# Decoder trunk: a pair's last product one place forward, the fourth-sum product first at second pairs, and a part's last modulation row moved into the next part

## The chip, the cores and the metric

One core of one Trainium2 chip runs the program. The metric is the device time of one execution in microseconds (us), lower being better; three timed executions of the kernel before lie between 1927.19 and 1928.88.

Names used for the engines: PE is TensorE (matrix products), DVE is VectorE, ACT is ScalarE, POOL is GpSimd, SP is SyncE, which here only issues transfers.

## The reference, cut to what matters

Two layers over x (512 tokens by 1024 features). Each layer is a half-step feed-forward block (FFN), a token mixer (a short gated convolution in layer 0, sparse attention in layer 1) and a second half-step FFN, so there are four FFNs. The change touches only the FFNs and the modulation rows that are computed beside them.

```python
def swiglu(h, w_in, w_out):
    g, u = jnp.split(h @ w_in, 2, axis=-1)
    return (jax.nn.silu(g) * u) @ w_out

cond = jax.nn.silu(c)
for i in range(DEPTH):
    mod = (cond @ ada_w[i] + ada_b[i]).reshape(bsz, 3, 3, D_MODEL)
    shift, scl, gate = mod[:, :, 0], mod[:, :, 1], mod[:, :, 2]
    h = adaln(x, norm_g[i, 0], shift[:, 0], scl[:, 0])
    x = x + HALF * gate[:, 0, None, :] * swiglu(h, ffn_w_in[i, 0], ffn_w_out[i, 0])
    ...  # the mixer, then the second FFN in the same way
```

`w_in` is 1024 by 5632 (gate and up halves of 2816 each), `w_out` is 2816 by 1024, and `ada_w` is 1024 by 9216 for each layer.

## The kernel before, in words

Every float32 product is made as three products of rounded float32r operands: `mm3` (L166 to L169) multiplies the high part of the weights by the high and by the low part of the activations, and the low part of the weights by the high part. An operand is split into its high and low part by `split` (L162 to L164): ACT writes the high part, and DVE subtracts it from the source for the low part. So each weight tile passes through ACT and then DVE (tiles `whi`, `wlo`; `qah`, `qal`; `qbh`, `qbl`; `qch`, `qcl`; `qdh`, `qdl`) before PE can use it.

An FFN (`ffn`, L620) works through the 22 column blocks of the hidden layer. A block j holds a gate column and an up column of 128 features, a *pair*. The blocks are cut into four *parts* (`FOUR`: blocks 0 to 5, 6 to 11, 12 to 17, 18 to 21). After a part's pairs, that part's share of the second matrix is multiplied (tiles `y`, weights `in_ffo`) and added to x, eight output rows d (L806); the last part does this in two halves (tiles `ty`).

A pair is computed by `seven_products` (L634): a scheme of Strassen's kind that makes the pair's four half-size blocks with seven half-size products. Each product is 4 `mm3`, 12 matmuls of 128x256. In program order a pair brings these, with the PSUM tiles `ox`, `oy`, `oz` and the copies of their sums into SBUF (`e`, `e3`):

1. first weights `a11` (tile `whi`/`wlo`) into `ox`, copied by ACT to `e`;
2. `before[0]()`, which is the *fourth* product of the pair before (`b4`, tiles `qdh`/`qdl`, into that pair's `oy`, then DVE L718 and ACT L719);
3. second weights `a12` (the other half of `whi`/`wlo`) into `oz`, added by DVE L705;
4. `b2` (`qbh`/`qbl`) into `ox` again, copied by ACT to `e` (the copy that the variable `copy` keeps);
5. `s1` (`qah`/`qal`) into `oy`, copied by ACT to `e3`;
6. `before[1]()`, the *last* product of the pair before (`c22`, tiles `qch`/`qcl`, into that pair's `ox`), then DVE L724 and L725, which read `ox` and make the pair's hidden activation `af`, and `keep`, which splits it (`ahi`, `alo`; `hid.done` holds the two instructions);
7. `s3` (`qah`/`qal`) into `ox`, added by DVE L714.

The first pair of a part has nothing to do at 2 and 6. The last pair's fourth and last products are made after the loop, among the first `y` products. At the second pair of a part (`second`, worked out in the loop of L756 on as "the block after the first one") the split of `whi` waits for the copy of the pair before (`issue_after`, L663).

The sums `qb` of DVE (L661, L662) are made from the raw weight tile `wraw` (3 buffers) and the accumulated tile `qa`; SP loads `wraw`, two halves of `qa` and `a22` for each pair (L647, L648, L656, L657), and POOL adds the fourth block to `qa` with an accumulating transfer (L654). A load waits until its buffer is free.

The modulation rows (`adaraw`, one row of `ada_w` for 128 features) are spread over the FFN: `each()` does the next one. It issues a 512 KB load into one of two buffers (L153, from POOL in these FFNs) and then `row_sum` on DVE (L147, an instruction of 128x1024 that multiplies by `cond` and sums, and one that reads the sum). Rows are asked for once before the `y` stage (`row()`) and after each output row d's addition L806 in the first three parts of an FFN (in the first FFN not in its first part, except d from 2 to 6). The fourth FFN has none.

Each engine runs its instructions in the order in which a scheduler has written them; the scheduler goes by program order, priorities and `issue_after`, and its order may differ from program order.

## Time and profile before

| what | value |
|---|---|
| median of three timed runs | 1927.41 us |
| the profiled execution's own time | 1933.05 us |
| its span, first to last instruction | 1931.3 us |
| PE busy | 1881.0 us (97%) |
| DVE busy | 1515.2 us (78%) |
| ACT busy | 950.9 us (49%) |
| POOL busy | 250.6 us (13%) |
| mean granted TensorE clock | 0.998 |
| transfers | 324.76 MB, mean 168 GB/s |
| chain of waits, shares | PE 74%, DVE 13%, DMA 7%, ACT 3% |

In a row of the timeline stand the start in us from the span's start, the duration, the engine, the line, the operation, output and inputs, and in brackets how long the engine was idle before it and what released it. The row of a wait gives the total in us, the number of times and the longest one. A row of a windows table gives busy time and number of instructions of PE, weight loads, DVE, ACT and POOL, then the granted clock, the transfer engines' share and GB/s.

### The profile page before, as it was taken

Reading aid. Unit: us, or ns where it says so; the run is one execution under the profiler, and the core shown is the slowest. Engines: PE = TensorE matmul, PEld = TensorE weight load, DVE = VectorE, ACT = ScalarE, POOL = GpSimd, SP = SyncE. Lnnn points to the kernel's source line nnn. Section 1 sums busy time; section 2 is a strip of 40 time slices with the busy share of each in tenths; the row PEclk is TensorE's granted clock in tenths of the full one; section 3 lists DMA queues with packets and bytes.
Section 4 is the critical chain, followed back from the end, with each engine's and each line's share of the span. In section 5 each row is a group of like instructions: output and inputs, shape, how many; then the busy total and the mean of one; then the engine's idle time right before and its main releaser. Section 6 shows DMA issues by size and latency. Waiting matters only on the chain.

```text
span 1931.3 us, 34417 instructions
## 1 busy us (share of the span) xinstructions
PE 1881.0 (97%) x13293; PEld 1742.4 (90%) x13293; DVE 1515.2 (78%) x2792; ACT 950.9 (49%) x1679; POOL 250.6 (13%) x346
## 2 busy tenths in 40 slices
PE   7999999999999999999999999999999999999999
PEld 5989898988899898989989898999888789898989
DVE  8976768888798777788878777787898988585765
ACT  3445353543236353535636353554788856363532
POOL 0010101000020111110011111000354620010100
PEclk9999999999999999999999999999999999999999
DMA  8576677457666676774567675324333325474741
GB/s 327 186 225 175 208 186 224 156 174 268 228 178 168 205 198 208 186 229 121 145 215 195 211 204 193 105 90 141 77 98 87 92 67 144 124 187 120 202 118 63
DMA packets 126673, 324.76 MB, mean 168 GB/s; under 512 B 15515, under 2 KB 16651, under 8 KB 126508
## 3 DMA queue, kind: packets, MB, share of 16 engines
q1 hardware_dynamic: 95196, 242.85, 38.5%
q0 software_dynamic: 31312, 79.71, 18.3%
q8 instruction: 104, 1.70, 0.4%
q14 instruction: 61, 0.50, 0.1%
HBM read 313.85 MB, written 3.15 MB: 164 GB/s over the span
## 4 chain that ended last, share of the span: by engine, by line
PE 74%; DVE 13%; DMA 7%; ACT 3%; issue 3%; SPq 1%; POOL 0%; DVEq 0%; ACTq 0%; POOLq 0%
PE gu L169 11%; PE gu L167 11%; PE gu L168 11%; PE y L167 5%; PE y L169 5%; PE y L168 5%; DMA adaraw<-in_adaw 2%; DVE wlo L164 2%; PE cv L167 2%; PE cv L168 2%; PE cv L169 2%; DMA wraw<-in_ffi 2%; PE ty L168 2%; PE ty L167 2%; PE ty L169 2%
## 5 line engine op out<-in xcount | busy, mean ns | idle before, releaser
L163 ACT ACTIVATE whi<-wraw 128x1024 fp32r<-128x1024 f32 (+2 forms) x261 | 252.9, 976 | 266.4 <-PE y L168 89.6
L164 DVE TENSOR_TENSOR wlo<-wraw,whi 128x1024 fp32r<-128x1024 f32 (+2 forms) x261 | 294.9, 1135 | 44.3 <-ACT whi L163 43.5
L169 PE MATMUL y<-ahi,wlo 128*128 128x512 f32 x576 | 224.3, 389 | 0.8 <-DVE wlo L164 0.8
L168 PE MATMUL y<-alo,whi 128*128 128x512 f32 x576 | 224.3, 389 | 0.0
L167 PE MATMUL y<-ahi,whi 128*128 128x512 f32 x576 | 224.3, 389 | 0.0
L147 DVE CUSTOM_DVE_ANT_0 adaraw<-adaraw,cond,adabs 128x1024 f32<-128x1024 f32 x144 | 185.2, 1303 | 40.3 <-DMA adaraw<-in_adaw 40.1
L169 PE MATMUL gu<-hhi,wlo 128*128 128x256 f32 x696 | 195.0, 280 | 14.1 <-DVE wlo L164 13.9
L167 PE MATMUL gu<-hhi,whi 128*128 128x256 f32 x696 | 193.8, 278 | 3.8 <-DVE af L725 3.8
L168 PE MATMUL gu<-hlo,whi 128*128 128x256 f32 x696 | 193.1, 278 | 0.0
L654 POOL DMA_DIRECT2D qa<-in_ffi x70 | 84.5, 1207 | 723.6 <-DMA qa<-in_ffi 248.0
L697 ACT ACTIVATE e<-gu 128x256 f32<-128x256 f32 x219 | 82.8, 378 | 168.4 <-PE gu L169 168.3
L167 PE MATMUL gu<-th,qah 128*128 128x256 f32 x584 | 161.4, 276 | 0.8 <-ACT e L697 0.8
L168 PE MATMUL gu<-tl,qah 128*128 128x256 f32 x584 | 161.3, 276 | 0.0
L169 PE MATMUL gu<-th,qal 128*128 128x256 f32 x584 | 161.3, 276 | 0.0
L169 PEld LDWEIGHTS gu<-hhi,wlo 128*128 128x128 f32 x696 | 131.1, 188 | 17.2 <-DVE wlo L164 17.2
L167 PEld LDWEIGHTS gu<-hhi,whi 128*128 128x128 f32 x696 | 131.1, 188 | 5.3 <-DVE af L725 4.8
L168 PEld LDWEIGHTS gu<-hlo,whi 128*128 128x128 f32 x696 | 131.0, 188 | 0.5
L169 PEld LDWEIGHTS y<-ahi,wlo 128*128 128x128 f32 x576 | 108.1, 188 | 24.2 <-DVE wlo L164 1.5
L167 PEld LDWEIGHTS y<-ahi,whi 128*128 128x128 f32 x576 | 108.2, 188 | 21.6
L168 PEld LDWEIGHTS y<-alo,whi 128*128 128x128 f32 x576 | 108.1, 188 | 21.6
L167 PEld LDWEIGHTS gu<-th,qah 128*128 128x128 f32 x584 | 109.7, 188 | 1.0 <-ACT e L697 1.0
L169 PEld LDWEIGHTS gu<-th,qal 128*128 128x128 f32 x584 | 109.7, 188 | 0.0
(327 smaller groups left out, 5753.8 us busy)
## 6 DMA issues: line engine op xcount, KB each, us to landing
wraw<-in_ffi SPq DMA_DIRECT2D x103, 512.0 KB, 4.7
adaraw<-in_adaw POOLq DMA_DIRECT2D x79, 512.0 KB, 4.8
qa<-in_ffi SPq DMA_DIRECT2D x146, 256.0 KB, 3.8
wraw<-in_ffo SPq DMA_DIRECT2D x96, 384.0 KB, 4.3
qa<-in_ffi POOLq DMA_DIRECT2D x70, 512.0 KB, 6.7
adaraw<-in_adaw SPq DMA_DIRECT2D x65, 512.0 KB, 4.6
a<-in_ffi SPq DMA_DIRECT2D x73, 256.0 KB, 4.4
wraw<-in_cwi SPq DMA_DIRECT2D x24, 512.0 KB, 4.5
```

What stands on the lines that cost most here:

```text
L147: return nc.vector.tensor_tensor_reduce(out=raw, in0=raw, in1=cond, scale=scale, scalar=adabs[:, c:c + 1], op0=ALU.mult, op1=ALU.add, accu ...
L163: act = nc.scalar.activation(hi, src, AF.Copy)
L164: return act, nc.vector.tensor_tensor(lo, src, hi, ALU.subtract)
L167: nc.tensor.matmul(o, sh, mh, start=first, stop=False, **kw)
L168: nc.tensor.matmul(o, sh, ml, start=False, stop=False, **kw)
L169: nc.tensor.matmul(o, sl, mh, start=False, stop=last, **kw)
L654: nc.gpsimd.dma_start(qa, bass.AP(tensor=a21.tensor, offset=a21.offset, ap=[a21.ap[0], [0, 2], a21.ap[1]]), accum_op=ALU.add)
L697: return nc.scalar.activation(to, o[:, lo], AF.Copy)
```

## The change

Three edits in `seven_products` and the loop that calls it:

- Products 5 and 6 change places: `before[1]()`, the last product of the pair before, comes ahead of `s1`. The split of `a22` into `qch`/`qcl`, which reuses the buffer that this product reads, goes with it.
- At a part's second pair, `before[0]()`, the fourth product of the first pair, comes ahead of product 1 in place of behind it.
- In parts whose rows follow every d, the row after d = 7 is not done there. Its d is put on a list `late`, and the row is done in the next part's second pair, after `before[1]()`, ordered behind the split of that pair's hidden activation. The number of rows stays the same. Eight rows are moved: two in the first FFN and three in each of the second and third; in the fourth, where no rows are left, the call does nothing.

```diff
--- before.py
+++ after.py
@@ -696,20 +696,27 @@
                     with tc.high_priority():
                         return nc.scalar.activation(to, o[:, lo], AF.Copy)
 
+                if second:
+                    before[0]()
                 product(ox[:, lo], a11, nrm.quarter(0, 0))
                 copied(e[:, 0], ox)
-                before[0]()
+                if not second:
+                    before[0]()
                 b4 = [sw.tile([P, QT], F32R, name=f"qd{e}") for e in "hl"]
                 split(qbs[1], *b4)
                 product(oz[:, lo], a12, nrm.quarter(1, 0))
                 nc.vector.tensor_tensor(e[:, 0], oz[:, lo], e[:, 0], ALU.add)
                 product(ox[:, lo], b2, t2, begin=False)
                 copy = copied(e[:, 1], ox)
+                before[1]()
+                if second and late:
+                    late.pop()
+                    with tc.issue_after(hid.done[1].ins):
+                        each()
+                c22 = [sw.tile([P, QT], F32R, name=f"qc{e}") for e in "hl"]
+                split(a22, *c22)
                 product(oy[:, lo], s1, t1)
                 copied(e3, oy)
-                before[1]()
-                c22 = [sw.tile([P, QT], F32R, name=f"qc{e}") for e in "hl"]
-                split(a22, *c22)
                 product(ox[:, lo], s3, t3, begin=False)
                 nc.vector.tensor_tensor(e3, ox[:, lo], e3, ALU.add)
 
@@ -761,7 +768,7 @@
                 for j in range(nj):
                     hid.activate(os[2 * j], os[2 * j + 1])
             held_back = []
-            copy = None
+            copy, late = None, []
             for p, (j0, j1) in enumerate(FOUR):
                 rest = none = (lambda: None,) * 2
                 for j in range(max(j0, nj), j1):
@@ -804,10 +811,12 @@
                             o = psum("y")
                             project(o, w, 0, a, [(k, k) for k in range(n)], True, True)
                         added = nc.vector.scalar_tensor_tensor(x[d], o, mod(s, 2, d), x[d], op0=ALU.mult, op1=ALU.add)
-                        if p or not first or 2 <= d < KD - 1:
+                        if (p or not first) and d == KD - 1:
+                            late.append(d)
+                        elif p or not first or 2 <= d < KD - 1:
                             with tc.issue_after(added.ins):
                                 each()
-            assert not todo
+            assert not todo and not late
             sw_es.close()
```

How this stands in the engines' orders is shown at three places. In the order after, the lines of the changed file are L708 for L705, L721 for L714, L725 for L718, L731 and L732 for L724 and L725, and L813 for L806. Buffer numbers are left out except where they tell rows apart.

**The second pair of the first FFN's third part.** DVE before, from the addition of the last output row d = 7 (L806) on; `adaraw` is the row, `wlo` in the sixth row the low part of the second pair's weights:

```order
L806 SCALAR_TENSOR_TENSOR x_85<-y,mods,x_85 128x512
L147 ISA adaraw,mods<-adaraw,cond,adabs 128x1024
L147 ISA mods 128x1
L705 TENSOR_TENSOR e<-gu,e 128x256
L164 TENSOR_TENSOR qbl<-qb,qbh 128x512
L164 TENSOR_TENSOR wlo<-wraw,whi 128x1024
L714 TENSOR_TENSOR e_2208<-gu,e_2208 128x256
```

DVE after, from the same addition on:

```order
L813 SCALAR_TENSOR_TENSOR x_85<-y,mods,x_85 128x512
L708 TENSOR_TENSOR e<-gu,e 128x256
L164 TENSOR_TENSOR qbl<-qb,qbh 128x512
L164 TENSOR_TENSOR wlo<-wraw,whi 128x1024
L721 TENSOR_TENSOR e_2205<-gu,e_2205 128x256
L164 TENSOR_TENSOR wlo<-wraw,whi 128x1024
```

The row no longer stands there, and `wlo` follows the addition after two rows. Further on in the same order of DVE after, with the first pair's L725 (now L732) at the top:

```order
L732 SCALAR_TENSOR_TENSOR af<-e,gu 128x256
L164 TENSOR_TENSOR qcl<-a_2283,qch 128x512
L164 TENSOR_TENSOR alo<-af,ahi 128x512
L147 ISA adaraw,mods<-adaraw,cond,adabs 128x1024
L147 ISA mods 128x1
L721 TENSOR_TENSOR e_2307<-gu,e_2307 128x256
```

The row has moved from ahead of the second pair's `wlo` to behind the split of the first pair's hidden activation (`alo`).

At the same place PE goes from the first pair's `s3` product (`qah`, `qal`) to the second pair. PE before:

```order
L167 MATMUL gu<-th_764,qah 128x256
L168 MATMUL gu<-tl_768,qah 128x256
L169 MATMUL gu<-th_764,qal 128x256
L167 MATMUL gu<-hhi_199,whi 128x256
L168 MATMUL gu<-hlo_201,whi 128x256
L169 MATMUL gu<-hhi_199,wlo 128x256
```

PE after, with `hhi_200`, `qdh` and `qdl` as the operands of the fourth product:

```order
L167 MATMUL gu<-th_764,qah 128x256
L168 MATMUL gu<-tl_768,qah 128x256
L169 MATMUL gu<-th_764,qal 128x256
L167 MATMUL gu<-hhi_200,qdh 128x256
L168 MATMUL gu<-hlo_202,qdh 128x256
L169 MATMUL gu<-hhi_200,qdl 128x256
```

In place of the second pair's first product, the first pair's fourth product follows.

**POOL between the same two parts.** POOL before, with the buffer numbers: `qa` loads are the accumulating transfers of the second and third pair, and `adaraw_2177` is the moved row, `adaraw_3034` and `adaraw_3041` the two rows after it:

```order
L654 DMA qa_2420<-in_ffi 128x2x512
L153 DMA adaraw_2177<-in_adaw 128x1024
L153 DMA adaraw_3034<-in_adaw 128x1024
L153 DMA adaraw_3041<-in_adaw 128x1024
L654 DMA qa_2555<-in_ffi 128x2x512
```

POOL after; the moved row is now numbered `adaraw_2384`:

```order
L654 DMA qa_2420<-in_ffi 128x2x512
L153 DMA adaraw_2384<-in_adaw 128x1024
L153 DMA adaraw_3034<-in_adaw 128x1024
L654 DMA qa_2555<-in_ffi 128x2x512
L153 DMA adaraw_3041<-in_adaw 128x1024
```

The moved row's load has kept its place, and of the two rows after it the second one's load has gone behind the next accumulating transfer.

**The third pair of the first FFN's second part.** DVE before, from the split of the first pair's hidden activation on; `qb<-qa,wraw` is L661's sum for the third pair, `qb<-qb,wraw` L662's, and `wlo` near the end belongs to the sixth pair:

```order
L164 TENSOR_TENSOR alo<-af,ahi 128x512
L714 TENSOR_TENSOR e_1265<-gu,e_1265 128x256
L661 TENSOR_TENSOR qb<-qa,wraw 128x512
L164 TENSOR_TENSOR qal<-qa,qah 128x1024
L662 TENSOR_TENSOR qb<-qb,wraw 128x512
L164 TENSOR_TENSOR qbl<-qb,qbh 128x512
L718 TENSOR_TENSOR e<-gu,e 128x256
L164 TENSOR_TENSOR qdl<-qb,qdh 128x512
L705 TENSOR_TENSOR e<-gu,e 128x256
L724 SCALAR_TENSOR_TENSOR af<-e,e_1265 128x256
L164 TENSOR_TENSOR wlo<-wraw,whi 128x1024
L725 SCALAR_TENSOR_TENSOR af<-e,gu 128x256
```

DVE after, from the same split on:

```order
L164 TENSOR_TENSOR alo<-af,ahi 128x512
L661 TENSOR_TENSOR qb<-qa,wraw 128x512
L662 TENSOR_TENSOR qb<-qb,wraw 128x512
L721 TENSOR_TENSOR e_1265<-gu,e_1265 128x256
L164 TENSOR_TENSOR qbl<-qb,qbh 128x512
L164 TENSOR_TENSOR qal<-qa,qah 128x1024
L725 TENSOR_TENSOR e<-gu,e 128x256
L164 TENSOR_TENSOR qdl<-qb,qdh 128x512
L731 SCALAR_TENSOR_TENSOR af<-e,e_1265 128x256
L708 TENSOR_TENSOR e<-gu,e 128x256
L164 TENSOR_TENSOR wlo<-wraw,whi 128x1024
L732 SCALAR_TENSOR_TENSOR af<-e,gu 128x256
```

The two sums L661 and L662 and the split `qbl` have moved ahead of the split `qal`, and L662, the last reader of the third pair's `wraw`, now comes second.

## Prediction

> **What bounds the kernel now.** I read the page first, then PE's waits, then the timeline of all engines around the longest of them, then windows for the granted clock.
>
> ```profile
> PE 1881.0 (97%) x13293; PEld 1742.4 (90%) x13293; DVE 1515.2 (78%) x2792; ACT 950.9 (49%) x1679; POOL 250.6 (13%) x346
> L167 PE MATMUL gu<-th,qah 128*128 128x256 f32 x584 | 161.4, 276 | 0.8 <-ACT e L697 0.8
> adaraw<-in_adaw POOLq DMA_DIRECT2D x79, 512.0 KB, 4.8
> ```
>
> PE is the bound, so only time in which PE stands still, or runs at a lower clock, can go. The change takes no matmul away. The second row counts the pairs: a pair has 8 such matmuls (four in `s1`, four in `s3`), so 584 are 73 pairs. They lie in 15 parts (16, less the first FFN's first, which uses another routine). The waits of PE in the pairs:
>
> ```profile
> PE gu L169 <- DVE wlo L164: 13.9, 14, 4.2
> PE gu L167 <- DVE af L725: 3.8, 4, 1.5
> PE gu L169 <- DVE qbl L164: 2.3, 2, 1.2
> PE gu L167 <- ACT e L697: 0.8, 1, 0.8
> ```
>
> The 14 waits of the first row are one at each second pair but that of the third FFN's first part, where the idle time is too short to be listed. The longest is at the first FFN's third part:
>
> ```profile
> 224.68 1.05 ACT L163 ACTIVATE whi<-wraw 128x1024 fp32r<-128x1024 f32 x1
> 225.63 0.37 ACT L697 ACTIVATE e<-gu 128x256 f32<-128x256 f32 x1
> 226.47 0.28 PE L167 MATMUL gu<-hhi,whi 128*128 128x256 f32 x1
> ...
> 223.29 0.75 DVE L806 SCALAR_TENSOR_TENSOR x<-y,mods,x 128x512 f32<-128x512 f32 x1
> 227.65 1.28 DVE L147 CUSTOM_DVE_ANT_0 adaraw<-adaraw,cond,adabs 128x1024 f32<-128x1024 f32 x1 [3.60 <-DMA adaraw<-in_adaw]
> 228.86 0.42 DVE L705 TENSOR_TENSOR e<-gu,e 128x256 f32<-128x256 f32 x1
> 229.19 0.68 DVE L164 TENSOR_TENSOR qbl<-qb,qbh 128x512 fp32r<-128x512 f32 x1
> 229.79 1.22 DVE L164 TENSOR_TENSOR wlo<-wraw,whi 128x1024 fp32r<-128x1024 f32 x1
> ...
> 231.06 0.38 PE L169 MATMUL gu<-hhi,wlo 128*128 128x256 f32 x1 [4.21 <-DVE wlo L164]
> ```
>
> The high part `whi` is ready at 225.73. DVE has ended the last addition at 224.04, but the next instruction in its order is the row's sum, and the row's load has not landed: 3.60 us idle, then 1.21 for the row, and only then L705, `qbl` and `wlo`. PE has begun the pair at 226.47 and stops at its third matmul, the first that reads `wlo`.
>
> **What such a wait costs.** The listed idle time is not all of it:
>
> ```profile
> 1687.60 0.28 PE L167 MATMUL gu<-th,qbh 128*128 128x256 f32 x1
> 1692.26 0.39 PE L169 MATMUL gu<-hhi,wlo 128*128 128x256 f32 x1 [0.19 <-DVE wlo L164]
> 1696.26 0.28 PE L167 MATMUL gu<-th,qbh 128*128 128x256 f32 x1
> 1705.78 0.28 PE L167 MATMUL gu<-th,qbh 128*128 128x256 f32 x1
> ```
>
> From the second to the third pair's `b2` product, with no wait, PE takes 1705.78 - 1696.26 = 9.52 us for seven products, so 1.36 for one. From the first to the second pair's there are six (no last product yet): 8.16, and 8.66 were taken. A wait listed with 0.19 costs 0.50: 0.31 on top, as the pipeline drains and starts again. And the clock:
>
> ```profile
> 231.00:235.00 4.00, 3.94 (x20) 3.94 (x21) 3.75 (x5) 0.39 (x1) 0.00 (x0) 0.58 0.72 242
> 672.00:676.00 4.00, 4.00 (x24) 4.00 (x23) 3.49 (x5) 1.02 (x2) 0.00 (x0) 0.58 0.70 205
> 767.00:769.00 2.00, 2.00 (x20) 2.00 (x19) 2.00 (x2) 0.98 (x2) 0.00 (x0) 1.00 0.72 242
> ...
> 670.82 0.38 PE L169 MATMUL gu<-hhi,wlo 128*128 128x256 f32 x1 [1.81 <-DVE wlo L164]
> 765.48 0.39 PE L169 MATMUL gu<-hhi,wlo 128*128 128x256 f32 x1 [2.71 <-DVE wlo L164]
> ```
>
> After the waits of 4.21 and 1.81 us the granted clock is 0.58 over 4 us, a loss of 4 x 0.42 = 1.7 each; after that of 2.71 it stays at 1.00. [...]
>
> **The change, part by part.**
>
> *The row, and the fourth product first at second pairs.* Both work on the same 14 waits. With the row gone, DVE at 224.04 does L705 (0.33 from start to start), then `qbl`, whose source is ready in time, and is free for `wlo` when `whi` is ready at 225.73; `wlo` ends by about 226.95. PE meanwhile has the first pair's fourth product, 1.36 us from 226.47, whose operands were split in the part before. It needs the copy of `oy` (225.63 to 226.00), so there is 0.47 us in hand. It reaches `wlo` at 226.47 + 1.36 + two matmuls, about 228.1, more than 1 us after it is ready. In parts without a row the 0.19 waits go for the same reason. The sum: 13.9 + 14 x 0.31 + 2 x 1.7 = 21.6 us, all saved. The check at the longest wait: 4.21 + 0.31 + 1.7 = 6.2.
>
> The row itself still costs DVE 1.21 us, now in the second pair. By the order on POOL its load keeps its place, so it has landed at 227.65; the row's sum now comes after the first pair's last product (fifth in the slot: 226.47 + 6.8 = 233.3), L725 0.34, `qcl` 0.60 and `alo` 0.60, at about 235, 7 us after the landing. What is queued behind it on DVE until the third pair's `qbl` is needed: 1.2 of the row, L714 0.34, L661 0.60, `qal` 1.13, L662 0.60, `qbl` 0.60 (steps of the rows below). From the end of the last product that makes 0.34 + 0.60 + 0.60 + 1.2 + 0.34 + 0.60 + 1.13 + 0.60 + 0.60 = 6.0 us, and PE needs `qbl` after two products to the slot's end and three of the next, 5 x 1.36 = 6.8. That fits with 0.8 us to spare, and costs nothing. On POOL, the row load that has moved behind the accumulating transfer is not needed before the next part.
>
> *The last product one place forward.* It needs `qcl` and, in `ox`, that L714 has read it:
>
> ```profile
> 142.23 0.28 PE L167 MATMUL gu<-hhi,whi 128*128 128x256 f32 x1
> ...
> 141.62 0.69 DVE L164 TENSOR_TENSOR qcl<-a,qch 128x512 fp32r<-128x512 f32 x1
> 142.23 0.69 DVE L164 TENSOR_TENSOR alo<-af,ahi 128x512 fp32r<-128x512 f32 x1
> 142.83 0.42 DVE L714 TENSOR_TENSOR e<-gu,e 128x256 f32<-128x256 f32 x1
> 143.17 0.69 DVE L661 TENSOR_TENSOR qb<-qa,wraw 128x512 f32<-128x512 f32 x1
> 143.77 1.22 DVE L164 TENSOR_TENSOR qal<-qa,qah 128x1024 fp32r<-128x1024 f32 x1
> 144.90 0.69 DVE L662 TENSOR_TENSOR qb<-qb,wraw 128x512 f32<-128x512 f32 x1
> ...
> 145.92 0.38 SPq L656 DMA_DIRECT2D wraw<-in_ffi  x1
> 150.92 1.06 ACT L163 ACTIVATE whi<-wraw 128x1024 fp32r<-128x1024 f32 x1 [1.31 <-DMA wraw<-in_ffi]
> 152.02 1.23 DVE L164 TENSOR_TENSOR wlo<-wraw,whi 128x1024 fp32r<-128x1024 f32 x1 [4.22 <-ACT whi L163]
> 153.16 0.41 DVE L725 SCALAR_TENSOR_TENSOR af<-e,gu 128x256 f32<-128x256 f32 x1
> ...
> 153.62 0.39 PE L167 MATMUL gu<-hhi,whi 128*128 128x256 f32 x1 [1.48 <-DVE af L725]
> ```
>
> In the slot that begins at 142.23 both are done by 143.25, 1.0 us in; the last product now starts 4 x 1.36 = 5.4 in. So 4.4 us cover it. What it brings lies in the waits for L725. There DVE's order has the sixth pair's `wlo` ahead of the second pair's L725, and that `wlo` waits for a load that could only be issued when L662 had freed its buffer. Now L662 comes one product (1.36 us) earlier with `alo`, and ahead of L714 and `qal` (1.47 us): about 142.8, and the load lands about 3 us earlier, at 147.9. But ACT has the split `qch` ahead of `whi`, which starts when the last product ends, now at 149.0: 0.6 for it, 1.05 for `whi`, 1.2 for `wlo`, 0.34 for L725 give about 152.3. PE comes at about 151.7 and loses 0.6 + 0.31 in place of 1.48 + 0.31: 0.9 saved. In the third part's like wait (the rest of the first FFN's two) the order after has L725 ahead of that `wlo`; there 1.6 goes, but the late `wlo` then delays the fourth pair's `qbl`, a new wait that I put at 0.9 + 0.31: 0.4 saved. The two waits for `qbl` (2.3 + 2 x 0.31 = 2.9) go, since `qal` (1.13) and one product (1.36) no longer stand ahead of it.
>
> ```profile
> 1636.20 0.84 ACT L163 ACTIVATE whi<-wraw 128x768 fp32r<-128x768 f32 x1 [3.48 <-DMA wraw<-in_ffo]
> 1637.37 0.38 PE L167 MATMUL gu<-th,qah 128*128 128x256 f32 x1 [0.78 <-ACT e L697]
> 1639.63 0.38 PE L167 MATMUL gu<-hhi,whi 128*128 128x256 f32 x1 [0.58 <-DVE af L725]
> ```
>
> The other two L725 waits and the one for ACT's copy hang on a load of `in_ffo` that lands when it did; PE only comes to it in another order. I take 0.8 of their 2.8. So this edit saves 0.9 + 0.4 + 2.9 + 0.8 = 5.0 us; its bounds are 0 and all seven waits, 6.9 + 7 x 0.31 = 9.1.
>
> **The sum.** 21.6 + 5.0 = 26.6 us: the profiled execution's 1933.05 would become 1906.4. It is 5.64 us longer than the median of the runs shown; the saving set against the median gives 1927.41 - 26.6 = 1900.8, and I take 1901. If all waits in the pairs went, 30.7 would be saved: 1896.7.
>
> **The rivals.** A measurement of this kernel can tell 0.2%, 3.85 us, from no change.
>
> *DVE is full at the third pairs.* The 0.8 us above assumes that ACT and the loads are in time. If they are 1.8 us late, PE waits 1 us + 0.31 at each of the eight third pairs that now follow a row: 10.5 us back, 1911. For it: DVE is 78% busy. Against it: now the row and its wait stand ahead of the same work of DVE, so that DVE comes to the third pair sooner after the change than before it.
>
> *The waits are longer under the profiler.* The 5.64 us by which the profiled execution is longer may be waits for loads that the timed runs don't have. Then 21 are saved: 1906. For it: they hang on loads; against: the span is otherwise steady PE work.
>
> *The wait moves with the row.* If the row's load were issued only behind the accumulating transfer, the 3.6 us idle would come again at the third pairs; less the 0.8 to spare and with 0.31 on top that is 3.1 us, 8 times: 25 us back, 1926, which can't be told from no change. The order on POOL speaks against it.
>
> *Slower: the last product waits at its new place.* It does so once in 73 - 15 = 58 slots. If `qcl` or L714 came more than 4.4 us later than in the row above, each slot would stop; at 0.53 us each the 26.6 and 3.85 are used up and it is slower, and at 0.6 the time is 1936. Nothing in the rows comes near.
>
> **How the numbers follow.** The forecast has a chance of 0.62, DVE full at the third pairs 0.14, waits longer under the profiler 0.13, the wait that moves 0.07, slower 0.04. The first three are faster by over 0.2%: 0.89; the fourth is within it, 0.07; slower 0.04. The range goes from 1896, all waits gone, to 1914, which holds the second rival and part of its sum with the third; some 2 in 10 are left out, most above.
>
> **What would show it.** Right: in PE's waits the row for `wlo` is gone or below 2 us; L147 in the second pairs shows no idle time for its load; the interval between the first two `b2` products of a part is 8.2 us; no clock of 0.58 at second pairs. Wrong: new rows of PE waiting for `qbl` or `qal` at third pairs, for `qcl` or L714 at the last product, for ACT's copy of `oy` at the fourth, or `wlo` waits with another releaser on DVE.

## The result, and the profile after

The changed kernel takes 1907.11 us (median of four executions, 1905.69 to 1908.68), the kernel before beside it 1927.3 (1922.06 to 1928.88): a ratio of 0.990, 95% interval 0.988 to 0.992. It is faster by 20.2 us, where 1901.0 had been forecast. The profiled executions differ by more: 1933.05 before, 1905.69 after, 27.4 us. The page after (busy time, share of the span, instructions):

```profile
PE 1871.5 (98%) x13293; PEld 1736.6 (91%) x13293; DVE 1516.9 (80%) x2792; ACT 951.1 (50%) x1679; POOL 250.5 (13%) x346
```

PE is still the bound. The waits of PE in the pairs (us in total, times, longest) are down to two kinds:

```profile
PE gu L167 <- ACT e L697: 2.5, 2, 1.4
PE gu L169 <- DVE qbl L164: 0.8, 1, 0.8
```

The 14 waits for `wlo` (13.9 us) and the four for the half of `af` are gone. The place of the longest of them, the second pair of the first FFN's third part, now looks like this (start, duration, instruction; L708 and L813 are the old L705 and L806):

```profile
219.29 1.05 ACT L163 ACTIVATE whi<-wraw 128x1024 fp32r<-128x1024 f32 x1
...
216.16 0.75 DVE L813 SCALAR_TENSOR_TENSOR x<-y,mods,x 128x512 f32<-128x512 f32 x1
217.26 0.42 DVE L708 TENSOR_TENSOR e<-gu,e 128x256 f32<-128x256 f32 x1 [0.36 <-PE gu L169]
219.15 0.69 DVE L164 TENSOR_TENSOR qbl<-qb,qbh 128x512 fp32r<-128x512 f32 x1 [1.47 <-ACT qbh L163]
220.38 1.23 DVE L164 TENSOR_TENSOR wlo<-wraw,whi 128x1024 fp32r<-128x1024 f32 x1 [0.53 <-ACT whi L163]
...
216.99 0.28 PE L167 MATMUL gu<-th,qbh 128*128 128x256 f32 x1
221.07 0.28 PE L167 MATMUL gu<-hhi,qdh 128*128 128x256 f32 x1
222.43 0.28 PE L167 MATMUL gu<-hhi,whi 128*128 128x256 f32 x1
222.66 0.28 PE L169 MATMUL gu<-hhi,wlo 128*128 128x256 f32 x1
```

Behind the last addition DVE goes straight to L708: the row's sum no longer stands there. `wlo` ends at 221.61, 4.62 us after the first pair's `b2` product began at 216.99; PE does the fourth product (`qdh`) at 221.07, and reads `wlo` first at 222.66. DVE now waits for ACT, and PE for nobody. The granted clock is the third number from the end in a row of the windows:

```profile
220.00:224.00 4.00, 4.00 (x37) 4.00 (x37) 3.62 (x4) 3.98 (x7) 0.00 (x0) 1.00 0.34 111
672.00:676.00 4.00, 4.00 (x37) 4.00 (x37) 3.72 (x7) 2.82 (x6) 0.05 (x1) 1.00 0.92 346
```

No second pair has a clock below 1.00 any more.

**A measure for all kernels.** The start of each pair's `b2` product (its first matmul `gu<-th,qbh`) gives 15 intervals from a part's first to its second pair, nominally 8.16 us, and 43 between later pairs, nominally 9.52. What they take beyond that is called *excess* below. Before it was 22.8 us at second pairs and 10.4 at the others; after, 0.35 and 5.9. So 22.4 + 4.5 = 26.9 of the 27.4 us lie in the pairs.

The other intervals did not all improve: in the first FFN's third part they are 11.06, 11.00 and 9.68 (before: 11.21, 9.56 and 11.17), and in the third FFN's first part 11.52 (before: 10.27). The two waits of PE in that third part, the last two rows here, with what stands ahead of them on DVE, SP and ACT:

```profile
229.23 0.69 DVE L164 TENSOR_TENSOR alo<-af,ahi 128x512 fp32r<-128x512 f32 x1
229.83 1.28 DVE L147 CUSTOM_DVE_ANT_0 adaraw<-adaraw,cond,adabs 128x1024 f32<-128x1024 f32 x1
...
231.37 0.68 DVE L661 TENSOR_TENSOR qb<-qa,wraw 128x512 f32<-128x512 f32 x1
231.97 1.22 DVE L164 TENSOR_TENSOR qal<-qa,qah 128x1024 fp32r<-128x1024 f32 x1
233.11 0.68 DVE L662 TENSOR_TENSOR qb<-qb,wraw 128x512 f32<-128x512 f32 x1
...
234.12 0.38 SPq L656 DMA_DIRECT2D wraw<-in_ffi  x1
...
240.82 1.06 ACT L163 ACTIVATE whi<-wraw 128x1024 fp32r<-128x1024 f32 x1 [2.66 <-DMA wraw<-in_ffi]
...
242.31 0.36 ACT L697 ACTIVATE e<-gu 128x256 f32<-128x256 f32 x1
...
242.72 0.38 PE L167 MATMUL gu<-hhi,qdh 128*128 128x256 f32 x1 [1.09 <-ACT e L697]
247.07 0.38 PE L169 MATMUL gu<-th,qbl 128*128 128x256 f32 x1 [0.84 <-DVE qbl L164]
```

The row's sum waits for no load now, but it stands on DVE ahead of L661 and L662; between these two stands the split `qal` (1.14 us), too. L662 frees the buffer of the weight tile, so SP issues the next load only at 234.12. ACT then stands at `whi` for 2.66 us, and the copy of `oy`, which PE needs for the fourth product, is queued behind it. So one of the signs that the prediction gave for being wrong did come: PE waiting for ACT's copy of `oy` at a fourth product, once, 1.09 us.

### The profile page after: what moved, and what is told of

The parts are those of the page before. It is cut to its first block, busy times and chain, and to the rows that moved or that the text cites. A ratio compares the mean times of both kernels' runs of the same rounds, so it can differ in the third digit from the quotient of the medians.

```text
span 1903.9 us, 34466 instructions
## 1 busy us (share of the span) xinstructions
PE 1871.5 (98%) x13293; PEld 1736.6 (91%) x13293; DVE 1516.9 (80%) x2792; ACT 951.1 (50%) x1679; POOL 250.5 (13%) x346
## 4 chain that ended last, share of the span: by engine, by line
PE 84%; DVE 8%; ACT 3%; DMA 2%; issue 2%; SPq 1%; DVEq 0%; ACTq 0%
PE gu L167 13%; PE gu L169 12%; PE gu L168 12%; PE y L167 7%; PE y L168 7%; PE y L169 7%; PE cv L167 2%; PE cv L169 2%; PE cv L168 2%; PE hs L168 2%; PE hs L169 2%; PE hs L167 2%; PE ty L168 2%; PE ty L169 2%; PE ty L167 2%
## 5 line engine op out<-in xcount | busy, mean ns | idle before, releaser
L164 DVE TENSOR_TENSOR wlo<-wraw,whi 128x1024 fp32r<-128x1024 f32 (+2 forms) x261 | 294.8, 1134 | 44.8 <-ACT whi L163 44.0
L167 PE MATMUL y<-ahi,whi 128*128 128x512 f32 x576 | 224.3, 389 | 0.0
L169 PE MATMUL y<-ahi,wlo 128*128 128x512 f32 x576 | 224.2, 389 | 0.0
L167 PE MATMUL gu<-hhi,whi 128*128 128x256 f32 x696 | 192.9, 277 | 0.0
L169 PE MATMUL gu<-hhi,wlo 128*128 128x256 f32 x696 | 192.5, 277 | 0.0
L167 PE MATMUL gu<-th,qah 128*128 128x256 f32 x584 | 161.5, 276 | 1.4 <-ACT e L697 1.4
L169 PE MATMUL gu<-th,qal 128*128 128x256 f32 x584 | 161.2, 276 | 0.0
L167 PEld LDWEIGHTS gu<-hhi,whi 128*128 128x128 f32 x696 | 130.7, 188 | 1.0 <-DVE af L732 0.4
L169 PEld LDWEIGHTS gu<-hhi,wlo 128*128 128x128 f32 x696 | 130.7, 188 | 0.0
L169 PEld LDWEIGHTS y<-ahi,wlo 128*128 128x128 f32 x576 | 108.1, 188 | 22.9
L167 PEld LDWEIGHTS y<-ahi,whi 128*128 128x128 f32 x576 | 108.2, 188 | 21.7
L167 PEld LDWEIGHTS gu<-th,qah 128*128 128x128 f32 x584 | 109.6, 188 | 1.6 <-ACT e L697 1.6
L169 PEld LDWEIGHTS gu<-th,qal 128*128 128x128 f32 x584 | 109.7, 188 | 0.0
```

The costliest lines, as they stand in the source:

```text
L164: return act, nc.vector.tensor_tensor(lo, src, hi, ALU.subtract)
L167: nc.tensor.matmul(o, sh, mh, start=first, stop=False, **kw)
L169: nc.tensor.matmul(o, sl, mh, start=False, stop=last, **kw)
```

## The experiments

All runs in one table: span and excess of the profiled execution, and the median of the timed ones, with the ratio to the kernel before run beside it. Spans less both excesses come to 1896 to 1901 in all rows, so excess is nearly all that differs.

| kernel | span | excess, second pairs | excess, others | median | ratio, 95% interval |
|---|---|---|---|---|---|
| before, first profile | 1931.3 | 22.8 | 10.4 | 1927.3 | |
| before again | 1931.8 | 22.8 | 10.9 | 1932.0 | 1.001 (0.999 to 1.003) |
| row moved only | 1915.2 | 8.4 | 10.7 | 1919.6 | 0.9936 (0.9913 to 0.9958) |
| fourth first only | 1920.1 | 7.4 | 14.0 | 1920.6 | 0.9941 (0.9919 to 0.9962) |
| last forward only | 1929.4 | 26.2 | 2.2 | 1920.7 | 0.9954 (0.9933 to 0.9974) |
| before, rows without loads | 1915.0 | 8.5 | 7.7 | 1918.4 | 0.9944 (0.9923 to 0.9964) |
| last and row | 1912.6 | 8.7 | 4.8 | 1913.9 | 0.9908 (0.9884 to 0.9932) |
| last and fourth | 1915.7 | 10.7 | 7.2 | 1910.8 | 0.990 (0.9877 to 0.9922) |
| after, first profile | 1903.9 | 0.35 | 5.9 | 1907.1 | 0.990 (0.988 to 0.992) |
| after again | 1905.7 | 0.9 | 6.1 | 1907.5 | 0.9876 (0.9851 to 0.990) |
| after, DVE work of the row doubled | 1904.0 | 0.5 | 7.6 | 1906.3 | 0.9885 (0.9861 to 0.9908) |
| row one pair later | 1901.5 | 0.7 | 3.9 | 1903.2 | 0.9861 (0.9836 to 0.9887) |
| the same again | 1900.3 | 0.4 | 3.1 | 1902.4 | 0.9865 (0.9839 to 0.9891) |
| row later, fourth not first at one place | 1902.9 | 0.9 | 4.4 | 1904.7 | 0.9871 (0.9846 to 0.9896) |

### The kernel before, once more

The edit is none.

> The kernel before, unchanged, run and profiled once more. The ratio of its time to that of the kernel before must come out at 1 and shows how wide an interval a null comparison has. The question is the profile. If the waits for wlo at the second pairs hang on row loads that land late or early from one execution to the next, the excess of the second-pair intervals over 8.16 us, which was 22.8 us in the first profile, comes out clearly smaller here: about 16 us, and the profiled time at about 1927 in place of 1933.05. If it is the profiler that makes these waits long, it comes again at 22 to 23 us and about 1933.

The ratio is 1.001 (0.999 to 1.003), so that a difference of less than some 4 us can't be told from none. The profile's waits for `wlo` came again:

```profile
PE gu L169 <- DVE wlo L164: 15.6, 15, 2.7
```

The sum is like the first (22.8 us of excess both times), but it lies elsewhere. The longest is 2.7, not 4.2; the second pair that took 14.31 us takes 10.87, that of the first FFN's fourth part 10.48 in place of 8.66, those of the third FFN 11.16, 9.37 and 10.80 in place of 9.81, 9.41 and 9.74. So where a wait is long is chance, and that there are such waits is not.

Of the two readings in the expectation, the first (16 us, about 1927) failed and the numbers of the second, the profiler's, came: 22.8 us and 1933.55. They do not show the profiler to be the cause, since the other executions of this same kernel, with nothing changed, took 1923.69 to 1940.75, and 1933 lies well within that. Nor is it ruled out: in all five profiles in which the rows stand at the old place and are loaded (before, before again, fourth first only, last forward only, last and fourth) the execution took 1.3 to 10.4 us longer than the median of its row in the table, in the nine others between 2.6 us less and 0.5 more. Whether profiling makes these waits longer stays open.

Over 63 other executions of the kernel before in this study the median is 1929.5, the range 1920.6 to 1941.0, and 19 are longer than the first profile's 1933.05. Of the 59 run beside the experiments, the nine with a mean granted clock of 1.000 have a median of 1922.6, the ten with 0.996 or less one of 1934.8. The eight executions of the changed kernel lie between 1904.2 and 1910.0, all at 1.000. The change takes away the scatter along with the time.

### Only the row moved

```diff
-                        if p or not first or 2 <= d < KD - 1:
+                        if (p or not first) and d == KD - 1:
+                            late.append(d)
+                        elif p or not first or 2 <= d < KD - 1:
...
                 before[1]()
+                if second and late:
+                    late.pop()
+                    with tc.issue_after(hid.done[1].ins):
+                        each()
```

> Only the row is moved: the last row of a part into the second pair of the next part, behind the last product where the kernel before has that. Theory (the row stands in DVE's order ahead of wlo and waits for its load): the eight second pairs that had a row, with 18.6 us of excess over 8.16 in the first profile, come down to the 0.5 to 0.7 us that the seven without a row show; 18.6 - 8 x 0.6 = 13.8 us saved against that profile, 7 to 10 us between the medians, since the medians of the whole change differ by 20.2 where the two profiles differ by 27.4. Rival (DVE is full): the row's 1.2 us come back as waits at the third pairs, 8 x 1.3 = 10.5 us, and nothing that can be measured is left.

```profile
PE gu L169 <- DVE wlo L164: 2.9, 15, 0.2
```

Each of the 15 second pairs is at 8.66 to 8.81, with a wait of 0.2: the eight with a row have become like the seven without one. Excess there went from 22.8 to 8.4, 14.4 us (expected 13.8), and the median by 9.2 (expected 7 to 10). The rival, DVE full at the third pairs, shows only faintly: the excess of the others goes from 10.4 to 10.7, and of the eight third pairs that follow a row the two in the first FFN wait 0.30 for `qbl` (intervals of 10.27 and 10.11); the six others are at 9.52.

### Only the fourth product first

```diff
+                if second:
+                    before[0]()
                 product(ox[:, lo], a11, nrm.quarter(0, 0))
                 copied(e[:, 0], ox)
-                before[0]()
+                if not second:
+                    before[0]()
```

> Only the fourth product is put first at second pairs. Theory (one product, 1.36 us, is cover for wlo): the seven second pairs without a row lose their whole excess, 4.2 us; of the eight with one, the five that were at 0.5 to 1.65 us lose all (5.7 us) and the three long ones 1.36 each (4.1 us): 14 us saved against the first profile, 10 to 13 between medians, and the three long ones still show 1.7 to 3 us or more. Rival (the wait only changes its place: the fourth product then waits for ACT's copy of oy or the DVE queue): the intervals stay at 8.6 or more and the time within 0.2% of before.

Waits of PE (L728 is the old L725):

```profile
PE gu L167 <- DVE af L728: 6.0, 9, 1.7
PE gu L169 <- DVE wlo L164: 4.1, 6, 1.3
```

Second pairs without a row are at 8.16 to 8.58, those with one at 8.17 to 9.78; excess falls by 15.4. The three that were longest in the first profile have 1.4, 1.1 and 0.4 us of excess left, less than the 1.7 to 3 expected; how late a row lands is not the same in two executions (the second pair of 14.31 us in the first profile of the kernel before took 10.87 in its second). But 3.6 us come back: five of the pairs that follow are at 10.17 to 10.26, waiting for the half of `af`, and the third FFN's first part is at 12.12 where it was 10.27. Between medians 8.2 us, less than the 10 to 13 expected. The fourth product first covers the wait and hands a part of it on, as long as the row stays where it was and the last product comes late.

### Only the last product forward

```diff
                 copy = copied(e[:, 1], ox)
+                before[1]()
+                c22 = [sw.tile([P, QT], F32R, name=f"qc{e}") for e in "hl"]
+                split(a22, *c22)
                 product(oy[:, lo], s1, t1)
                 copied(e3, oy)
-                before[1]()
-                c22 = [sw.tile([P, QT], F32R, name=f"qc{e}") for e in "hl"]
-                split(a22, *c22)
```

> Only the last product is put one place forward. Theory: the seven other waits in the pairs shrink (forecast 5.0 us saved; the profile of the whole change shows 4.5), the second pairs stay as they are: 4 to 5 us saved, about 1923, with the new waits at the third part of the first FFN and the first of the third FFN. Rival (the last product waits at its new place for qcl or for L714): 0.53 us in each of up to 58 slots, so slower.

```profile
PE gu L169 <- DVE wlo L164: 15.4, 14, 3.2
PE gu L167 <- ACT e L697: 0.4, 1, 0.4
```

Every wait for the half of `af` and for `qbl` is gone: the other intervals have 2.2 us of excess in place of 10.4. That is 8.2 saved, not 4 to 5, and 8.1 between medians. The first FFN's third part is at 9.51 to 9.53 in the intervals where the changed kernel has 11.06 and 11.00: the new waits there are not this edit's. The second pairs keep their waits. The rival, a stop at the new place, does not occur.

### Two edits of three

The edits are those above, in pairs.

> The last product forward and the row moved, without the fourth product first. Theory: second pairs as with the row alone, 8.66 to 8.8, excess 8.4 us; of the other slots the first FFN's third part shows 11.06 and 11.00 again (3.2 us), since the row is to blame there, and the third FFN's first part is at 10.2 as without the fourth product first: others about 5.4 us. About 17 us saved between medians, the sum of the two alone (9.2 and 8.1). Rival for the third part (the fourth product's place is to blame): others at 2.2 us, and about 20 saved.

> The last product forward and the fourth first, the row left where it was. Theory: the second pairs without a row at 8.16 to 8.3, those with a row at 8.2 to 9.8 with excess of 4 to 8 us in sum, as with the fourth alone; the first FFN's third part at 9.52 (no row in its slots), the third FFN's first part at 11.5 to 12. Savings between medians about 16 us, the sum of the two alone (8.2 and 8.1). Rival: the first FFN's third part still shows 11: then the fourth product is to blame for it.

With the row and without the fourth product first, the first FFN's third part is at 10.42, 10.76 and 10.62; the row is to blame there. The third FFN's first part is at 11.08, neither the 10.2 expected nor the 11.52 of the changed kernel. Between medians 16.3 us (expected 17).

With the fourth product first and the row in its old place, that third part has 11.44, 9.52 and 9.52: the expectation of 9.52 in all three failed in the first of them, which is the 11 that the rival had named, so the row is not alone in it there. PE waits for ACT's copy behind a late load there, too. The second pairs still have 10.7 us of excess, more than the 4 to 8 expected, since one took 12.17. Between medians 19.3 us (expected 16).

The edits overlap: alone they bring 9.2, 8.2 and 8.1, in sum 25.5, together 20.2 to 22.7. On top of the last product (8.1) the row is worth 8.2 more, the fourth product 11.2, and both together 14.6, not 19.4. Each of these numbers is uncertain by some 4 to 5 us, so that medians alone would not show the overlap. The profiles do: with the last product forward, the excess at second pairs is 26.2, with the row besides 8.7, with the fourth product besides 10.7, with both 0.35 and 0.9. The row takes 17.5 of it and the fourth product 15.5, 33 in sum, but together no more than 26: these two work on the same waits.

### The row without its load

```diff
+        if loads[0]:
+            queue.dma_start(raw, adaw[s * NADA + t])
+        row_sum(raw, s, t // KD, t % KD, None if loads[0] else cond)
...
+                            loads[0] = d < KD - 1
                             with tc.issue_after(added.ins):
                                 each()
+                            loads[0] = True
```

> The kernel before, with the eight last rows of the parts left without their load: the sum L147 stands at the same place on DVE and takes as long, but reads cond in place of a loaded row with a factor of 0, so these eight columns of mods hold their bias alone (the modulation of those rows is left out). Theory (DVE stands still at the sum because its load has not landed): the eight second pairs with a row, 18.6 us of excess in the first profile, come down to 0.5 to 1.0 each, 4 to 8 us in sum, with no granted clock under 0.9 there, and the executions lie closer together than the 20 us that those of before span; about 1916 to 1920, as with the row moved. Rival (it is the 1.2 us of DVE's work in front of wlo): the second pairs stay where they were, 1928 to 1932.

```profile
PE gu L172 <- DVE wlo L167: 2.9, 15, 0.2
```

L172 and L167 are the old L169 and L164. The DVE order is that of the kernel before and the row's 1.2 us still stand in front of `wlo`, yet all second pairs are at 8.67 to 8.87. It is the load that PE waits for, not DVE's work. The median is 1918.4 (1916.0 to 1921.9): with the loads goes the scatter, too.

### The row one pair later

The row's place in the second pair is taken out, and in the third pair it follows the two sums:

```diff
-                        nc.vector.tensor_tensor(qbs[1], qbs[0], raw[:, 1], ALU.add)
+                        summed = nc.vector.tensor_tensor(qbs[1], qbs[0], raw[:, 1], ALU.add)
+                    if late and j == max(j0, nj) + 2:
+                        late.pop()
+                        with tc.issue_after(summed.ins):
+                            each()
```

> The changed kernel with one thing different: the deferred row comes one pair later, behind the sums L661 and L662 of the part's third pair, instead of ahead of them in the second. Theory: the 3.2 us that the changed kernel loses in the first FFN's third part (slots of 11.06, 11.00 and 9.68 us in place of 9.52) come from the row standing on DVE ahead of L662, so that the next weight load is issued late; they go, the second pairs stay at 8.16, the other slots stay (11.52 and 9.94 at the first parts of the third and fourth FFN): excess of the other slots 5.9 to 2.7 us, about 1904 where the changed kernel run beside it has 1907. Rival: those slots are slow because of the fourth product's place or the loads alone: nothing changes, 5.9 us and 1907. Second rival (DVE is full at third pairs): the row now delays qal and qbl of the third pair by 1.2 us, new waits for qbl in up to eight slots, over 1907.

> The version with the row one pair later, once more, for its interval: 1902 to 1905, the first FFN's third part at 9.52 in its third and fifth slots, and within 0.7 us of it in the fourth, which showed 10.12 the first time.

> The changed kernel, unchanged, run and profiled once more beside the others: 1905 to 1909, second pairs at 8.16 to 8.3, the same two new places of waiting (the first FFN's third part, the third FFN's first) as in its first profile. If those two places are chance of one execution, they differ here.

DVE and SP in the third pair of the first FFN's third part, first profile:

```profile
230.46 0.68 DVE L164 TENSOR_TENSOR alo<-af,ahi 128x512 fp32r<-128x512 f32 x1
231.06 0.68 DVE L661 TENSOR_TENSOR qb<-qa,wraw 128x512 f32<-128x512 f32 x1
231.78 0.69 DVE L662 TENSOR_TENSOR qb<-qb,wraw 128x512 f32<-128x512 f32 x1
232.39 0.42 DVE L721 TENSOR_TENSOR e<-gu,e 128x256 f32<-128x256 f32 x1
232.72 1.28 DVE L147 CUSTOM_DVE_ANT_0 adaraw<-adaraw,cond,adabs 128x1024 f32<-128x1024 f32 x1
...
232.50 0.33 SPq L656 DMA_DIRECT2D wraw<-in_ffi  x1
...
237.46 1.06 ACT L163 ACTIVATE whi<-wraw 128x1024 fp32r<-128x1024 f32 x1 [0.71 <-PE gu L169]
```

From `alo` to the issue of the load it is 2.0 us, where the changed kernel has 4.9, and `whi` no longer waits for the load (0.80 in the second profile, at no cost to PE). Not all of the 2.9 is the row's 1.2. With the row's place the written order has changed around it: the split `qal` (1.1) and L721 (0.3) now come behind L662, too, and SP issues this load ahead of two `qa` halves in place of behind them. The load itself is also done sooner: `whi` starts 6.7 us after the issue in the changed kernel, at its load's landing, and no more than 5.0 here. So the run shows that the row's place makes these waits, and not how much of it is the row's own time.

The intervals there are 9.52, 10.12 and 9.52, and 9.52 in all three in the second run. No wait for `qbl` has come. One place is new in all three profiles with the row there: in the first FFN's second part, where no row is moved, the interval from the fourth to the fifth pair is 10.64, 10.09 and, in the last run below, 10.87, where the changed kernel has 9.52; PE waits 0.3 to 1.1 us for ACT's copy, which is queued behind a `whi` that waits for its load.

Beside it in the same run the changed kernel has its two new places again: 11.20, 10.76 and 10.67 in the first FFN's third part, 11.46 in the third FFN's first. The medians are 1903.2 and 1907.5 there; over all runs ten executions of this version have a median of 1902.9 and eight of the changed kernel one of 1907.4. Seven of the ten lie below the lowest of the eight (1904.24). The intervals of the ratios to the kernel before overlap, since that kernel scatters by 20 us; 4.5 is what the medians show. The 3.2 us expected are borne out in the part for which they were named (excess 3.2 before, 0.6 and 0.0 here); over all the other intervals 2 to 3 us go (5.9 and 6.1 before, 3.9 and 3.1 here). This is the fastest version seen.

### The DVE work of the row doubled

```diff
         row_sum(raw, s, t // KD, t % KD)
+        if more[0]:
+            nc.vector.tensor_tensor(raw, raw, raw, ALU.add)
```

> The changed kernel with DVE's work for each deferred row doubled: behind each of the eight sums one more DVE instruction over the same 128x1024 buffer, about 1.15 us, whose result nobody reads. Theory: in the second and third FFN the operands of the next pair are made a slot ahead and it is hidden; in the first FFN it stands, like the row, in front of L662 and of the weight load that hangs on it, so the third part's slot of 11.06 to 11.20 grows by about 1.2 to 12.3, and one or two beside it; 1908 to 1911 in all. Rival (DVE is full at the third pairs): 8 x (1.15 + 0.31) = 11.7 us, about 1919.

PE's waits (L173 is the old L169):

```profile
PE gu L173 <- DVE qbl L168: 2.5, 9, 0.4
```

Both were wrong, the theory in its places and the rival in its size. The third part's interval is 11.24, no longer than without (11.06 and 11.20), though its load is issued 6.0 us after `alo` in place of 4.9; why that costs nothing stays open. The second and third FFN do not hide it: in their six parts with a deferred row one interval, between the third and the fourth pair, is at 10.00 to 10.32, 0.5 to 0.8 us each, as is that of the first FFN's fourth part (10.11). The waits are for the third pair's `qbl`, where the rival had put them, but of 0.2 to 0.4 us. So one row fits, and 1.15 us more do not. That agrees with the 0.8 us to spare of the prediction: 1.15 - 0.8 leaves 0.35, and with the 0.31 on top of a wait 0.66 us. The time does not show it (1906.3), because others of the intervals that depend on loads were shorter in this run (10.38 in place of 11.52 in the third FFN).

### The fourth product not first at the third FFN's first part

The condition `second` of that edit becomes `second and (p or s != 3)`, in the version with the row one pair later.

> The version with the row one pair later, and the fourth product first at all second pairs but that of the third FFN's first part. Theory: there the early fourth product only brings PE sooner to the wait for ACT's copy, which stands on ACT behind a split whose load lands when it did: the slots of 8.59 and 11.54 there become about 8.8 and 10.3, 0.6 to 1.0 us saved, which the times cannot tell. Rival (the fourth product's place has nothing to do with it): 11 or more in the second of the two slots again.

The two intervals are 8.79 and 10.68, in sum 19.47; with the fourth product first they were 8.59 and 11.54, and 8.28 and 11.53 in its two runs, 20.13 and 19.81. So 0.3 to 0.7 us, the right sign and too little to be sure of; the second did not come down to 10.3. What sets it stands on ACT in the changed kernel:

```profile
941.12 0.84 ACT L163 ACTIVATE whi<-wraw 128x768 fp32r<-128x768 f32 x1 [4.33 <-DMA wraw<-in_ffo]
941.87 0.37 ACT L697 ACTIVATE e<-gu 128x256 f32<-128x256 f32 x1
...
942.29 0.39 PE L167 MATMUL gu<-th,qah 128*128 128x256 f32 x1 [1.38 <-ACT e L697]
```

The copy is queued behind a split that waits for its load. Whether an earlier load would cure it was not tried, and the time of the whole kernel (1904.7, against 1903.2 and 1902.4) shows no gain from this edit.

## Why the prediction was right, and where it was not

*The row and the fourth product: right, in mechanism and in size.* Forecast 21.6 us, measured 22.4 of excess at second pairs. The working at the longest wait held almost to the hundredth: `wlo` was to end at 226.95 with the pair's `b2` product at 222.38, 4.57 later, and did so 4.62 later; PE was to reach it at 228.1, 5.72 later, and did so after 5.67. That the load is the cause, and not the 1.21 us of the row, is shown by the kernel without loads. DVE's own idle time before the row sums tells the same; the last two numbers in its row of the page are all the idle time and that for the load, first before, then after:

```profile
L147 DVE CUSTOM_DVE_ANT_0 adaraw<-adaraw,cond,adabs 128x1024 f32<-128x1024 f32 x144 | 185.2, 1303 | 40.3 <-DMA adaraw<-in_adaw 40.1
```

```profile
L147 DVE CUSTOM_DVE_ANT_0 adaraw<-adaraw,cond,adabs 128x1024 f32<-128x1024 f32 x144 | 185.6, 1305 | 12.9 <-DMA adaraw<-in_adaw 12.6
```

*"That fits with 0.8 us to spare, and costs nothing": half right.* For `qbl` it held, as the doubled row shows from the other side: one row fits, two do not. But the step counted only what PE needs from DVE. L662, behind the row, is also what releases a weight buffer, and in the first FFN's third part the load that hangs on it was issued 2.9 us later, part of it the row's 1.2 and part the order that came with it. With the row behind L662 the two waits there go. The forecast had one of them, "the late `wlo` then delays the fourth pair's `qbl`, a new wait that I put at 0.9" (measured 0.84), and it came as it was put, behind a `wlo` that waits for its load. But the forecast booked it to the last product's move; with that edit alone it does not come (9.52 there), and the load is late because of the row.

*The last product one place forward: 5.0 forecast, 4.5 measured, from other parts.* Alone it is worth 8.2, near the bound of 9.1. In the first FFN's second part it saves 3.8 where some 2.4 had been put (0.9 and one of the two `qbl` waits). The step that failed is "ACT has the split `qch` ahead of `whi`":

```profile
140.58 0.69 DVE L662 TENSOR_TENSOR qb<-qb,wraw 128x512 f32<-128x512 f32 x1
...
141.30 0.33 SPq L656 DMA_DIRECT2D wraw<-in_ffi  x1
...
146.40 1.06 ACT L163 ACTIVATE whi<-wraw 128x1024 fp32r<-128x1024 f32 x1 [1.77 <-DMA wraw<-in_ffi]
147.63 0.62 ACT L163 ACTIVATE qch<-a 128x512 fp32r<-128x512 f32 x1
...
148.64 0.41 DVE L732 SCALAR_TENSOR_TENSOR af<-e,gu 128x256 f32<-128x256 f32 x1
...
150.14 0.28 PE L167 MATMUL gu<-hhi,whi 128*128 128x256 f32 x1
```

In the changed kernel `whi` is ahead of `qch` on ACT, as it is in the kernel before (150.92 and 151.89 there), and starts when its load lands; L732, the old L725, is done 1.1 us before PE comes. The load itself landed when the forecast had it, at 147.9: the two profiles are 1.61 us apart here (by the second pair's `b2` product), and 146.40 + 1.61 is 148.0. In the third part the row gives the gain back: 0.2 saved where 0.4 and the other `qbl` wait (1.5) had been put. At the third and fourth FFN's first parts 1.25 was lost and 1.6 gained, 0.35 in sum for a forecast of 0.8.

*The sum: right against the profile, wrong against the median.* 26.6 forecast, 27.4 measured: 1906.4 was the forecast for the profiled execution and 1905.69 its time. The step that failed is "the saving set against the median gives 1927.41 - 26.6 = 1900.8, and I take 1901". The waits that the change removes are the very thing by which executions of the kernel before differ. The profile held 27.4 us of them, the median execution 20 to 23 (1927.3 to 1930.1 against 1907.1 to 1907.5); what is left once they are gone is nearly the same in each execution, so it is the profile less its own waits that forecasts it. The rival "the waits are longer under the profiler" had the right number, 1906. Its reason is not needed, since the kernel before, run again, gave 1933.55 in its profile and up to 1940.75 in the other executions; it is not ruled out either, as said at that run. That 1905.69 came within 0.7 of 1906.4 is in part luck: one term was 0.8 us too small and the other 0.5 too large, and the second came from other places than forecast.

*The other rivals.* With one row PE nowhere waits for `qbl` at a third pair in the changed kernel; the wait did not move with the row (none of the eight moved sums has idle time ahead of it on DVE, the one at 229.83 among them); and the last product never waits at its new place in the kernel with that edit alone.

## What to carry to other kernels

When an instruction in an engine's order waits for a load, look at what stands behind it (here `wlo`, behind a sum at which DVE stood still for 3.60 us), and move it to where its load is surely there; but look also at which buffer the instructions behind the new place release, since a weight load can hang on them (here one was issued 2.9 us later). Where executions scatter, subtract removed waits from the execution in which they were counted, not from a median. Price an edit with the others in place: here two edits that each took 15 us or more of the same waits took no more than 26 together, and moving one of the three by one pair gave 4 more.

## What the runs showed of the hardware

**Clock after short waits.** In the kernel with the last product forward a wait of 2.37 us and one of 3.21 us, both in front of steady work, were answered differently:

```profile
664.00:668.00 4.00, 2.04 (x11) 2.04 (x12) 4.00 (x6) 1.57 (x2) 0.53 (x1) 0.81 0.58 153
668.00:672.00 4.00, 4.00 (x29) 4.00 (x28) 2.96 (x5) 1.34 (x3) 0.00 (x0) 0.76 0.80 250
...
1104.00:1108.00 4.00, 1.21 (x11) 1.01 (x9) 3.00 (x5) 3.20 (x5) 0.53 (x1) 1.00 0.10 23
1108.00:1112.00 4.00, 3.58 (x30) 3.58 (x31) 4.00 (x5) 1.01 (x2) 0.00 (x0) 1.00 0.78 246
1112.00:1116.00 4.00, 4.00 (x37) 4.00 (x37) 3.60 (x9) 3.01 (x5) 0.00 (x0) 1.00 0.62 199
...
665.96 0.39 PE L169 MATMUL gu<-hhi,wlo 128*128 128x256 f32 x1 [2.37 <-DVE wlo L164]
1108.42 0.38 PE L169 MATMUL gu<-hhi,wlo 128*128 128x256 f32 x1 [3.21 <-DVE wlo L164]
```

Over the 8 us from 664 on, around and after the shorter wait, the granted clock is 0.81 and 0.76, a loss of 4 x 0.19 + 4 x 0.24 = 1.7 us, the same that the prediction worked out; around and after the longer one it stays at 1.00. So the length of the wait alone does not decide here whether the clock falls, nor in the kernel before, where it fell after a wait of 1.81 us and not after one of 2.71. What does was not shown.

**Around a short wait.** The starts of PE's matmuls around the wait of 0.19 us at 1692.26 in the kernel before:

```profile
1691.68 0.28 PE L167 MATMUL gu<-hhi,whi 128*128 128x256 f32 x1
1691.79 0.28 PE L168 MATMUL gu<-hlo,whi 128*128 128x256 f32 x1
1692.26 0.39 PE L169 MATMUL gu<-hhi,wlo 128*128 128x256 f32 x1 [0.19 <-DVE wlo L164]
1692.48 0.28 PE L167 MATMUL gu<-hhi,whi 128*128 128x256 f32 x1
1692.60 0.28 PE L168 MATMUL gu<-hlo,whi 128*128 128x256 f32 x1
```

Without a wait they start 0.11 to 0.12 us apart and are listed with 0.28 each, so they overlap. Across the wait two starts are 0.47 apart, and the next is 0.22 later: 0.36 + 0.11 = 0.47 us more, of the 0.50 by which the interval is longer. So nearly all of the 0.31 that the prediction put on top of a listed wait is lost at the stop itself.

**Loads.** In the kernel before, PE's wait behind one and the same row load was 4.21 us in the first profile and 2.44 in the second, and 0.19 and 1.99 at the next. Without these eight loads, and nothing else changed, seven executions lie within 6 us of each other, where twelve of the kernel before in one run span 17, and 63 in all span 20. With all loads kept and the row moved, six lie within 5. That speaks for DVE's standing still at the sum, and not for the load, as what scatters the time.
